# Background copies, marks and one set of sums handed to the POOL queue in a one-core hybrid attention layer

## The chip, the core and the metric

The kernel runs on one core of a Trainium2 chip. The metric is device time in microseconds (us) for one execution of the whole layer. TensorE (PE) does the matmuls and the transposes, VectorE (DVE) and ScalarE (ACT) do elementwise work, GpSimd (POOL) does little but issue transfers, and SyncE (SP) does nothing but issue transfers. Every engine takes its own instructions strictly in its own order. Sixteen DMA engines move the bytes; the profile lists them under two main queues: what SP issues is `q1 hardware_dynamic`, what POOL issues is `q0 software_dynamic`.

## What is computed

One decoder layer on 512 tokens and a model width of 2048, all in float32:

```python
h = _rms_norm(x, g_pre)
proj = h @ w_in                                  # 2048 x 6472
(q_lat, kv_lat, k_rope_raw, gate_mla,
 fq, fk, fv, f_logit, gate_fox) = jnp.split(proj, split_points, axis=-1)
o_mla = _mla_branch(q_lat, kv_lat, k_rope_raw, g_q, w_uq, g_kv, w_ukv, cos, sin) * jax.nn.silu(gate_mla)
o_fox = _fox_branch(fq, fk, fv, f_logit, b_forget) * jax.nn.silu(gate_fox)
o = jnp.concatenate([o_mla, o_fox], axis=-1) @ w_out    # 2048 x 2048
return x + _rms_norm(o, g_post)
```

`_fox_branch` is causal attention with eight heads of 128 and a forget bias. `_mla_branch` is the latent attention: eight heads whose queries come from a normed latent of width 768 through `w_uq` and whose keys and values come from a normed latent of width 512 through `w_ukv`. The projections are the bulk of the work.

## The kernel before

**Exact products from three passes.** A float32 operand is split in two parts, `hi` and `lo` (`split_into`, L134 to L145; for weights `divide`, L272 to L283: ACT casts the high part at L279, DVE subtracts it at L282). A product is three matmuls, `hi*hi`, `hi*lo` and `lo*hi` (`mm3`, L148 to L152). Weights come in chunks of 128x1024 float32 (512 KB); chunk number i is loaded by `load`, split by `divide` and used by PE. `chunk(i)` is called by a product for each chunk in turn: it loads up to four chunks ahead (six in the latent heads) and divides up to two ahead. Raw chunks lie in three buffers in the latent heads and in six in the last products; `whi` and `wlo` have three buffers each.

**Seven products instead of eight.** The large projections (values, latents, gates, the value part of `w_ukv`, and `w_out`) are cut in blocks of 2x2, and sums and differences of weight blocks let seven block products do the work of eight. The sums of weights are called t7, t5, t6 and t4. They are made by transfers, not by an engine: a copy of one block from DRAM to a scratch tensor in DRAM, and then a transfer that adds the second block to it. A few sums are not made ahead. For these ("late"), `load` fetches the two blocks into two tiles, `raw` and `second` (L250), and `join` (L265 to L270) adds them on DVE just ahead of the split. For `w_out` the late one is t5, used by the products `g5`, 0 and `g5`, 1 in four chunks each.

**The background list.** `bg` holds the sums to be made, in order: eight narrow ones (512 KB) for the values, eight for the latents, eight for the gates, four for the value part of `w_ukv`, and twelve wide ones (1 MB, t7, t6 and t4 for four blocks) for `w_out`. `paced` (called by a product at each 128-row step of a chunk, "tile" in this text) counts tiles; each time the count reaches the pace (twice the pace for a wide sum) it calls `add_step(n)`, which does three things: it adds the second block to sum n-1 (POOL, L320), copies the first block of sum n (SP, L324), and writes a mark, 16 numbers out of the weight tile that PE is about to use, into the place of sum n+1 (SP, L326). The mark orders the copy of n+1 behind it, and so keeps the background work in step with the matmuls. In this kernel SP's queue holds the loads of `raw` (L242 and L259), the copies, the marks and the fetches of operands (L985), in one order.

**The latent heads** (L1590 on, `for p in range(4)`). For each p: `mla_q(p)` (six tiles, three PSUM banks of tag `pj`, of which there are four), then at p 0 the first of the products for the values, `up_product("p1", ...)`, into two banks `A`, then `mla_k(p)` (four tiles, two banks of `pj`), then scores and values of two heads. Steps of attention are queued in `todo` and are interleaved with the matmuls by `pump`. At p 2 operand blocks a11 and a12 of the output projection are fetched, at p 3 they are divided (`divisions`, at the head of `todo`). After the loop the a11 blocks of the last four heads' part are split (`head_steps(j, ("a11",), ...)`, j 2 and 3), and the output projection begins with the product `p1`, 0. Its products run in the order p1, p1, p2, p4, p4, q6, g5, g7, q6, g5, g7, g3, g3, p2 (block column 0 or 1); the order of the instructions on each engine is settled by a scheduler when the kernel is built.

**Scratch slots.** `slot` takes one of 28 general buffers of 4 KB per partition; operands, gates, and in the output projection also the `second` tiles are kept there.

Of the kernel before, what the change touches and what calls it, by code (L numbers as in the profile page):

```python
# [16 lines left out]
ALU = mybir.AluOpType  # L17
# [49 lines left out]
def tile_hybrid_layer(  # L67
# [16 lines left out]
    nc = tc.nc  # L84
    pe, act, dve, pool = nc.tensor, nc.scalar, nc.vector, nc.gpsimd
# [14 lines left out]
    def slot(name, dt=F32, shape=(P, 2, S)):  # L100

        return sp.tile(list(shape), dt, tag="s", name=name)

    def bank(tag, name, bufs):
        return ps.tile([P, 512], F32, tag=tag, name=name, bufs=bufs)

    def proj_bank(name):
        return bank("pj", name, 4)
# [23 lines left out]
    def in_order(*instructions):  # L132

        for i in instructions:  # L134
            tc.keep_in_program_order(i)
# [88 lines left out]
    def raw_tile(i):  # L224
        if deep and deep[1] <= i < deep[2] and (i - deep[1]) % (DEEP + 3) < DEEP:
            return deep[0].tile([P, 1024], F32, tag="raw", name=f"raw{i}", bufs=DEEP)
        if i in up_chunks:
            return slot(f"raw{i}", shape=(P, 1024))
        if i <= prods["g7", "v"][-1] and i % 5 < 2:
            return vr.tile([P, 1024], F32, tag="raw", name=f"raw{i}", bufs=2)  # L230
        pool = more[0] if more and (i - more[1]) % 6 < 3 else wp
        return pool.tile([P, 1024], F32, tag="raw", name=f"raw{i}", bufs=3)

    def load(i, small=None):

        w, cols, k, n, width = chunks[i]
        assert state["step"] >= needs.get(i, -3) + 2
        if cols is None:

            raw = raw_tile(i)  # L240
            for a, b in alike(raw, w):
                nc.sync.dma_start(a, b)  # L242
            raws[i] = raw
            if k is not None:
                if seconds:
                    pool, bufs = seconds
                    second = pool.tile([P, 2, 512], F32, tag="second", name=f"second{i}", bufs=bufs)
                else:
                    second = slot(f"second{i}")
                nc.sync.dma_start(second, k)  # L250
                raws[i] = raw, second.rearrange("p k c -> p (k c)")
            return
        if i < 2:
            raw = slot(f"raw{i}", shape=(P, 1024))
        else:
            raw = raw_tile(i)
        v = raw[:, : n * width].rearrange("p (k c) -> p k c", k=n)
        for at, off, cnt in cols:
            (nc.sync if cnt >= P or small is None else small).dma_start(  # L259
                v[:, :, at : at + cnt],  # L260
                w[0, k * P : (k + n) * P, off : off + cnt].rearrange("(k p) c -> p k c", p=P),
            )
        raws[i] = raw
# [41 lines left out]
    bg = []  # L305

    def alike(to, w):

        if len(w.shape) == 4:
            to = to.rearrange("p (k h x) -> p k h x", k=2, h=4)  # L310
            return [(to[:, k], w[:, k]) for k in range(2)]
        return [(to if len(w.shape) == 2 else to.rearrange("p (k c) -> p k c", k=2), w)]

    def add_step(n, mark):


        if n > 0:
            to, _, second = bg[n - 1]
            for a, b in alike(to, second):
                pool.dma_start(a, b, accum_op=ALU.add)  # L320
        if 0 <= n < len(bg):
            to, first, _ = bg[n]
            for a, b in alike(to, first):
                nc.sync.dma_start(a, b)  # L324
        if n + 1 < len(bg):
            nc.sync.dma_start(bg[n + 1][0][0:1, 0:16], mark)  # L326

    def sum_blocks(g, block, late, width=512, nj=4):

# [14 lines left out]
    prods = {}  # L344
# [62 lines left out]
    for n in ("q0", "p1", "k0", "p2", "q6", "p4", "g7", "q1", "g5", "k1", "g3", "q2", "k2", "q3", "k3"):  # L407
# [5 lines left out]
        p = int(n[1])  # L413
# [128 lines left out]
    todo = deque()  # L542
# [9 lines left out]
    def drain():  # L552
        while todo:
            todo.popleft()()

    def set_pace(n):
        state.update(pace=n, tiles=0)
# [378 lines left out]
    def head_steps(j, names, raw_of, place):  # L936

        return operand_steps("o", j, (o_of[K1[j]], o_of[K2[j]]), names, raw_of, place)
# [49 lines left out]
    def part_fetched(n, of, j):  # L988
        both = oper[n, of][j]
        split_into(both[:, 0], both[:, 1], both[:, 1].bitcast(F32), pin=True)  # L990

    def divisions(n, of):
        return [lambda j=j: part_fetched(n, of, j) for j in range(2 if of == "o" else 4)]
# [144 lines left out]
    def x_block(half, tokens):  # L1138
        def parts(kk, t):
            ts = slice((tokens + t) * P, (tokens + t + 1) * P)  # L1140
            return hh[8 * half + kk][:, ts], hl[8 * half + kk][:, ts]

        return parts
# [10 lines left out]
    def scaled_copy(to, o, t0, col=hcol):  # L1154
        for t in range(2):
            act.mul(to[:, t, :], o[t], col[:, t0 + t : t0 + t + 1])
# [28 lines left out]
    def v_block(name):  # L1185
        return vr.tile([P, 2, S], F32, tag="c", name=name)

    def v_out(c, tokens, half):

        for i in range(2):  # L1190
            to = v_away[2 * half + i].rearrange("p (t c) -> p t c", t=NT)[:, 2 * tokens : 2 * tokens + 2, :]
            pool.dma_start(to, c[:, :, 256 * i : 256 * (i + 1)])

    def two_of(make, name):
        return [make(f"{name}{i}") for i in range(2)]
# [24 lines left out]
    todo.extend([*fs[13:], *rot[:3]])  # L1220
    A = two_of(proj_bank, "va")
    product("p1", "v", x_block(0, 0), A, True, True)
    drain()
    pa, pb = v_block("vpa"), v_block("vpb")
    scaled_copy(pa, A, 0, rcol)
    scaled_copy(pb, A, 2, rcol)
    todo.extend([*x_steps(0), *x_steps(1)])
    fox_g(1, two_of(proj_bank, "fg1"))
    drain()
    todo.extend(rot[3:10])  # L1230
    product("p2", "v", x_block(1, 0), A, False, True)
    drain()
    c11 = v_block("vc11")
    scaled_copy(c11, A, 0, rcol)
    v_out(c11, 0, 0)
# [17 lines left out]
    k = fox_k(0, wholes)  # L1253
# [27 lines left out]
    for p in range(4):  # L1281
        if p:
# [6 lines left out]
            k = fox_k(p, wholes)  # L1289
# [138 lines left out]
    A, A2 = ([proj_bank(f"g{n}{t}") for t in range(2)] for n in "lm")  # L1428
# [102 lines left out]
    def halves(a):  # L1531
        return [a[:, t, :] for t in range(2)]
# [55 lines left out]
    for p in range(4):  # L1588
        q, qw, wholes = mla_q(p)
        if p == 0:  # L1590
            set_pace(3)
            A = two_of(proj_bank, "uA")
            up_product("p1", latent_x(0, 0), A, True)
            p1 = slot("up1")
            for t in range(2):
                act.copy(p1[:, t, :], A[t])
            p1 = halves(p1)
        elif p == 1:
            G = two_of(proj_bank, "uG")
            up_product("g5", operand("g5", "u"), G, True)  # L1600
            sub(up[1, 1], G, halves(up[1, 1]), ALU.add)
        elif p == 2:
            for f in (*fetches("a11", "o"), *fetches("a12", "o")):
                f()
        else:
            todo.extendleft([*divisions("a11", "o"), *divisions("a12", "o")])
        k, kw = mla_k(p, wholes)
        drain()
        heads = [
            Head(  # L1610
                f"m{2 * p + i}", q[i], k[i], None,
                lambda h=2 * p + i: gm[h],
                list(zip(qw[i], kw[i])),
            )
            for i in range(2)
        ]
        enqueue_scores(heads)
        if p == 0:
            up_product("p2", latent_x(1, 0), A, False)
            up[0, 0] = slot("u11")  # L1620
            for t in range(2):
                act.copy(up[0, 0][:, t, :], A[t])
            C = two_of(proj_bank, "uC")
            up_product("q6", operand("q6", "u"), C, True)
            up[0, 1] = slot("u12")
            sub(up[0, 1], C, p1)
            B = two_of(proj_bank, "uB")
            up_product("p4", latent_x(1, 2), B, True)
            up[1, 0] = slot("u21")
            sub(up[1, 0], B, p1, ALU.add)  # L1630
            up_product("g7", operand("g7", "u"), C, False)
            sub(up[1, 0], halves(up[1, 0]), C)
            up[1, 1] = slot("u22")
            sub(up[1, 1], C, p1)
            drain()
        elif p == 1:
            up_product("g3", operand("g3", "u"), G, False)
            sub(up[0, 1], G, halves(up[0, 1]), ALU.add)
        mla_values(p)
# [103 lines left out]
        nc.sync.dma_start(gp[c], g_post[:, out_cols(c)].to_broadcast([P, 512]))  # L1743


    for j in (2, 3):
        for s in head_steps(j, ("a11",), tmp, part_slot):
            s()
    todo.extendleft(head_steps(2, ("a12",), tmp, part_slot))
    A, A2 = ([proj_bank(f"oa{g}{t}") for t in range(2)] for g in range(2))  # L1750
    p1 = [slot(f"p1{g}") for g in range(2)]
# [106 lines left out]
```

## Time and profile before

| what | value |
|---|---|
| median of 3 runs | 903.24 us (901.15 to 906.73) |
| the profiled execution's own time | 902.74 us |
| its span, first to last instruction | 900.7 us |
| PE busy | 883.2 us, 98% of the span, 4486 matmuls |
| DVE busy | 659.6 us, 73% |
| ACT busy | 462.4 us, 51% |
| POOL busy | 72.8 us, 8%, 92 instructions |
| mean granted TensorE clock | 0.994 |
| q1 (SP's transfers) | 184.19 MB, 63.0% of 16 engines' span |
| q0 (POOL's transfers) | 39.85 MB, 21.6% of 16 engines' span |

A busy line gives the time of an engine, its share of the span and its instructions. In a table of stretches each row gives a stretch in us from the span's start, its length, the busy time of each engine with its number of instructions, the granted TensorE clock, the DMA engines' busy share, and GB/s. A row of waits names who waited for whom, with the total, the number of times and the longest, in us. A row of the chain of waits gives start, length and what the end of the kernel hung on at that time.

### The profile page before, as it was taken

The numbers are of one execution on the slowest core, as the hardware profiler recorded it, in microseconds if no ns is written. First come the engines' busy times: TensorE is split into PE (matmuls) and PEld (weight loads), VectorE is DVE, ScalarE is ACT, GpSimd is POOL, SyncE is SP. The second block draws the span as 40 slices with busy tenths as digits, with TensorE's granted clock in tenths as the row PEclk, the third lists the DMA queues.
The fourth block names the chain that finished last, engine by engine and source line by source line (L and its number), as shares of the span: only waits on it lengthen the run. The fifth ranks groups of instructions, "written<-read, shape, count | busy, mean of one in ns | idle before, by whom it ended". The sixth has DMA issues, their size and how long they took to land.

```text
span 900.7 us, 12696 instructions
## 1 busy us (share of the span) xinstructions
PE 883.2 (98%) x4486; PEld 749.3 (83%) x4486; DVE 659.6 (73%) x1106; ACT 462.4 (51%) x841; POOL 72.8 (8%) x92
## 2 busy tenths in 40 slices
PE   9999999999999999999999999999989999999996
PEld 9988888888888888889998998778868888877885
DVE  4679995458556545586588898979757895988786
ACT  6944443334343433435545565558454776636383
POOL 0110110001212111000000000000000000000021
PEclk9999999999999999999999999999989999999999
DMA  9998799889999998896899884799995137789879
GB/s 315 283 268 241 201 357 290 249 215 307 286 264 254 261 218 228 240 255 156 312 411 354 315 314 128 173 279 245 227 204 153 61 107 224 239 310 315 263 216 254
DMA packets 139235, 225.07 MB, mean 250 GB/s; under 512 B 16898, under 2 KB 68892, under 8 KB 138148
## 3 DMA queue, kind: packets, MB, share of 16 engines
q1 hardware_dynamic: 124660, 184.19, 63.0%
q0 software_dynamic: 13776, 39.85, 21.6%
q8 instruction: 35, 0.57, 0.2%
q10 hardware_dynamic: 736, 0.22, 0.1%
q14 instruction: 28, 0.23, 0.1%
HBM read 209.53 MB, written 69.22 MB: 309 GB/s over the span
## 4 chain that ended last, share of the span: by engine, by line
PE 85%; DVE 6%; DMA 5%; ACT 2%; issue 1%; SPq 0%; DVEq 0%; ACTq 0%
PE fq L150 3%; PE fk L150 3%; PE fk L152 3%; PE fk L151 3%; PE fq L152 3%; PE fq L151 3%; PE in L612 3%; PE fg L150 3%; PE fg L152 3%; PE fg L151 3%; PE sm L655 2%; PE oa L152 2%; PE sf L655 2%; PE oa L150 2%; PE oa L151 2%; DVE wlo L282 2%
## 5 line engine op out<-in xcount | busy, mean ns | idle before, releaser
L282 DVE TENSOR_TENSOR wlo<-raw,whi 128x1024 fp32r<-128x1024 f32 (+3 forms) x220 | 260.8, 1188 | 142.5 <-ACT whi L279 135.5
L279 ACT CAST whi<-raw 128x1024 fp32r<-128x1024 f32 (+3 forms) x220 | 224.4, 1023 | 242.5 <-PE fk L151 35.3
L150 PE MATMUL fk<-h,whi 128*128 128x512 f32 x128 | 52.5, 410 | 0.0
L150 PE MATMUL fq<-h,whi 128*128 128x512 f32 x128 | 50.8, 397 | 0.0
L150 PE MATMUL fg<-h,whi 128*128 128x512 f32 x128 | 50.3, 393 | 0.0
L152 PE MATMUL fk<-h,wlo 128*128 128x512 f32 x128 | 50.2, 392 | 0.0
L151 PE MATMUL fk<-h,whi 128*128 128x512 f32 x128 | 50.1, 392 | 0.0
L152 PE MATMUL fq<-h,wlo 128*128 128x512 f32 x128 | 50.0, 390 | 0.0
L151 PE MATMUL fq<-h,whi 128*128 128x512 f32 x128 | 49.9, 390 | 0.0
L152 PE MATMUL fg<-h,wlo 128*128 128x512 f32 x128 | 49.9, 390 | 0.0
L151 PE MATMUL fg<-h,whi 128*128 128x512 f32 x128 | 49.8, 389 | 0.0
L673 ACT ACTIVATE pf<-pf,stf 128x128 f32<-128x128 f32 (+3 forms) x32 | 18.0, 563 | 61.5 <-DVE stf L664 61.5
L269 DVE TENSOR_TENSOR raw<-raw,second 128x1024 f32<-128x1024 f32 x32 | 39.0, 1218 | 1.8 <-DMA second<-in_w_out_dram 1.8
L612 PE MATMUL in<-whi,h 128*128 128x328 f32 x128 | 30.0, 321 | 0.0
L150 PE MATMUL mq<-ln,whi 128*128 128x512 f32 x72 | 29.8, 417 | 0.0
L151 PE MATMUL mq<-ln,whi 128*128 128x512 f32 x72 | 28.9, 402 | 0.0
L152 PE MATMUL mq<-ln,wlo 128*128 128x512 f32 x72 | 28.9, 401 | 0.0
L152 PEld LDWEIGHTS fk<-h,wlo 128*128 128x128 f32 x128 | 24.0, 188 | 5.5
L152 PEld LDWEIGHTS fq<-h,wlo 128*128 128x128 f32 x128 | 24.0, 188 | 5.3
L152 PEld LDWEIGHTS fg<-h,wlo 128*128 128x128 f32 x128 | 24.0, 188 | 5.1
L151 PEld LDWEIGHTS fg<-h,whi 128*128 128x128 f32 x128 | 24.1, 188 | 4.8
L150 PEld LDWEIGHTS fg<-h,whi 128*128 128x128 f32 x128 | 24.0, 188 | 4.7
(610 smaller groups left out, 2416.5 us busy)
## 6 DMA issues: line engine op xcount, KB each, us to landing
raw<-in_w_in_dram SPq DMA_DIRECT2D x96, 512.0 KB
raw<-in_w_out_dram SPq DMA_DIRECT2D x32, 512.0 KB
second<-in_w_in_dram SPq DMA_DIRECT2D x24, 512.0 KB
bmg<-awaymg SPq DMA_DIRECT2D x20, 256.0 KB
awaymg<-rmg POOLq DMA_DIRECT2D x8, 512.0 KB, 7.5
raw<-t6v SPq DMA_DIRECT2D x8, 512.0 KB
t7o<-in_w_out_dram SPq DMA_DIRECT2D x4, 1024.0 KB
t7o<-in_w_out_dram POOLq DMA_DIRECT2D x4, 1024.0 KB, 10.8
```

Of the source, the lines that this page charges most:

```text
L150: pe.matmul(o, ah, bh, start=first, stop=False, **kw)
L151: pe.matmul(o, ah, bl, start=False, stop=False, **kw)
L152: pe.matmul(o, al, bh, start=False, stop=last, **kw)
L269: tc.keep_in_program_order(dve.tensor_tensor(out=raw, in0=raw, in1=second, op=ALU.add))
L279: cast = act.copy(hi[:, :m], raw[:, :m])
L282: dve.tensor_tensor(out=lo[:, :m], in0=raw[:, :m], in1=hi[:, :m].bitcast(F32), op=ALU.subtract)
L612: pe.matmul(banks[t][:, :n], a[k][:, tss[t]], b[:, j, :], start=k == 0 and m == 0, stop=k == NK - 1 and m == 2,)
L655: pe.matmul(s[:, :nn], a[:, qs], c[:, :nn], start=(i == 0), stop=(i == len(pairs) - 1))
L673: act.activation(p, p, AF.Exp, bias=st[:, 0:1], scale=unit, accum_out=st[:, 1:2])
```

## The change

Five edits:

1. The copies of the background list (L324) and the marks (L326) are issued by POOL, where the adds (L320) are already; SP keeps the loads and the fetches.
2. For the eight chunks of `g5`, 0 and `g5`, 1 of `w_out` the second block is no longer loaded into a tile of its own and joined on DVE. A transfer issued by POOL adds it to `raw` in SBUF.
3. In the latent heads the pace goes from 3 to 4.5 tiles, which for the wide sums is a step every nine tiles in place of six.
4. At p 0 the second bank of `A` is the `pv` bank in place of a second `pj` bank.
5. The splits of a11, j 2 and 3, move from behind the loop over p to the head of `todo` at p 3, ahead of the divisions.

```diff
@@ load
-            if k is not None:
+            if k is not None and i >= prods["g5", 0][0]:
+                in_order(nc.gpsimd.dma_start(raw.rearrange("p (k c) -> p k c", k=2), k, accum_op=ALU.add))
+            elif k is not None:
                 if seconds:
                     pool, bufs = seconds
@@ add_step
             for a, b in alike(to, first):
-                nc.sync.dma_start(a, b)
+                pool.dma_start(a, b)
         if n + 1 < len(bg):
-            nc.sync.dma_start(bg[n + 1][0][0:1, 0:16], mark)
+            pool.dma_start(bg[n + 1][0][0:1, 0:16], mark)
@@ for p in range(4)
         if p == 0:
-            set_pace(3)
-            A = two_of(proj_bank, "uA")
+            set_pace(4.5)
+            A = [proj_bank("uA0"), bank("pv", "uA1", 1)]
             up_product("p1", latent_x(0, 0), A, True)
@@ the same loop, p 3
-            todo.extendleft([*divisions("a11", "o"), *divisions("a12", "o")])
+            todo.extendleft(
+                [
+                    *divisions("a11", "o"), *divisions("a12", "o"),
+                    *(s for j in (2, 3) for s in head_steps(j, ("a11",), tmp, part_slot)),
+                ]
+            )
@@ behind the loop
-    for j in (2, 3):
-        for s in head_steps(j, ("a11",), tmp, part_slot):
-            s()
     todo.extendleft(head_steps(2, ("a12",), tmp, part_slot))
```

## The prediction, made before the change was run

> **What bounds the kernel now.** First the page: who is busy, and what the end hung on.
>
> ```profile
> PE 883.2 (98%) x4486; PEld 749.3 (83%) x4486; DVE 659.6 (73%) x1106; ACT 462.4 (51%) x841; POOL 72.8 (8%) x92
> ...
> PE 85%; DVE 6%; DMA 5%; ACT 2%; issue 1%; SPq 0%; DVEq 0%; ACTq 0%
> ```
>
> PE is idle for 900.7 - 883.2 = 17.5 us. No matmul is removed, so the change can win only what PE loses to waits, and whatever a lower clock costs after a wait. The second view is who PE waits for.
>
> ```profile
> PE ptm L682 <- DVE stm L664: 4.2, 1, 4.2
> ...
> PE uA L150 <- ACT mw L127: 1.0, 1, 1.0
> PE oa L152 <- DVE boa L140: 0.9, 1, 0.9
> ```
>
> One wait of 4.2 us stands out. It lies in the latent heads. Short stretches around it show that it costs more than its length:
>
> ```profile
> 668.70:673.20 4.50, 0.29 (x4) 0.06 (x2) 1.79 (x4) 1.09 (x2) 0.81 (x1) 0.75 1.11 217
> 673.20:677.70 4.50, 4.50 (x12) 3.65 (x13) 2.83 (x8) 3.16 (x9) 0.00 (x0) 0.50 0.96 197
> ```
>
> PE does nothing for 4.5 - 0.29 = 4.2 us, and for the next 4.5 us it is busy at a granted clock of 0.50, which loses another 2.25 us. Together **6.5 us**. The chain of waits tells why:
>
> ```profile
> 647.94 8.02 DMA t4o<-whi
> 655.98 0.56 SPq L324
> 656.59 0.61 SPq L259
> 657.25 12.99 DMA raw<-in_w_ukv_dram
> 670.34 1.05 ACT whi L279
> 671.41 1.23 DVE wlo L282
> 672.64 0.47 DVE pm L664
> ```
>
> Read it upward. PE waits for the softmax step pm on DVE. DVE stands in its own queue behind a weight split (wlo), that behind a cast, that behind the load of a `w_ukv` chunk. The load was issued at 656.6 and 657.2, behind the background copy (L324) in SP's queue, which stood until a mark (t4o<-whi) had landed, 8.02 us after its issue. And the load then took 12.99 us, with the 1 MB copy ahead of it in the same queue. The third view is SP's own waits:
>
> ```profile
> SPq L259 <- DVE wlo L282: 218.2, 77, 10.2
> ...
> SPq L326 <- ACT whi L279: 62.9, 23, 8.7
> ```
>
> SP mostly waits for raw buffers (218.2 us, harmless while loads are early enough), but 62.9 us go to marks whose weight tile is not yet cast, and every load stands behind them.
>
> **The change part by part.** The sum is made against the profiled execution's own 902.74 us; it stands 0.5 us under the median of 903.24.
>
> *Copies and marks to POOL, a step every nine tiles.* The list has 40 sums, so 40 marks and, as four of the copies take two transfers, 44 copies go from SP to POOL. The nearest price is that of the adds that POOL issues now:
>
> ```profile
> L320 POOL DMA_DIRECT2D t7o<-in_w_out_dram x4 | 4.7, 1163 | 52.2 <-DMA raw<-in_w_uq_dram 28.7 <-DMA t7o<-in_w_out_dram 23.5
> ```
>
> 84 x 1.16 = 97 us on an engine that is busy for 72.8 of 900; all of it lies beside PE. What counts is the load at 656.6. Was its buffer free earlier?
>
> ```profile
> 652.24 0.95 DVE L282 TENSOR_TENSOR wlo<-raw,whi 128x768 fp32r<-128x768 f32 x1
> ```
>
> With three raw buffers the load waits for the split of the chunk three before it, which by its shape (768 wide, a query chunk) is this one; it ends at 653.2. So the load can go at 653.3 and 653.9, 3.3 us earlier. It landed at 657.25 + 12.99 = 670.2, and PE resumed 2.9 us later, at 672.64 + 0.47 = 673.1, after its wait of 4.2; so a landing by 666 costs nothing, and 12 us are left. Even at the old 12.99 it would be 0.9 late, and no copy stands ahead of it any more. I take the whole 6.5 as won; the bounds are 3.3 and 6.5. What is late next is the same load, should it land after 666.
>
> The pace: after the first product of p 0 sets it, the loop has 48 tiles left (14 at p 0, 14 at p 1, 10, 10) and five steps to do. They took 30 tiles, to the second tile of p 2; they will take 45, to the last key tiles of p 3, past 700.
>
> ```profile
> 700.00:720.00 20.00, 20.00 (x102) 16.97 (x101) 17.10 (x42) 14.34 (x36) 0.00 (x0) 1.00 0.17 57
> ...
> 756.88 12.68 SPq L242 DMA_DIRECT2D raw<-t4o  x8
> ```
>
> There the DMA engines have room (0.17), and t4, the last sum and the first one read, is loaded from 756.9 on. So the slower pace costs nothing by itself, and it takes copies out of the full stretch; cover gone would mean an add later than 756, some 40 us off.
>
> *The pv bank at p 0.* A[1] no longer waits for a query bank to be emptied: 1.0 us (the uA row). The first mk product then takes query banks that are free sooner than the third, whose rotation it awaited too:
>
> ```profile
> PEld mk L150 <- DVE rbq L886: 0.5, 1, 0.5
> ```
>
> The pv bank is idle until the first values, after the products are over. **1.4 us** won of 1.5; bounds 0 and 1.5.
>
> *The sum of t5 by transfers into SBUF.* It takes eight loads of `second` off SP and eight joins off DVE. What it loses now is seen in matmuls per 20 us, and what the DMA engines have left in the last column but one:
>
> ```profile
> 780.00:800.00 20.00, 20.00 (x90) 16.57 (x89) 18.05 (x23) 10.27 (x14) 0.00 (x0) 1.00 0.76 248
> 800.00:820.00 20.00, 18.56 (x80) 14.36 (x79) 16.77 (x18) 9.78 (x12) 0.00 (x0) 1.00 0.87 288
> 820.00:840.00 20.00, 20.00 (x90) 16.57 (x89) 17.48 (x21) 9.12 (x14) 0.00 (x0) 1.00 0.95 349
> 840.00:860.00 20.00, 19.94 (x89) 16.02 (x88) 13.17 (x15) 8.94 (x9) 0.00 (x0) 1.00 0.87 281
> ```
>
> Ten matmuls of 90 are missing at 800 to 820: 10 x 20/90 = 2.2 us; one at 840 to 860, 0.2. The reason in the chain: the first `second` lands late, and then join, cast and the next join follow each other at 3.6 us a chunk, where PE takes 12 x 20/90 = 2.7.
>
> ```profile
> 785.10 5.68 SPq L242 DMA_DIRECT2D raw<-in_w_out_dram  x3
> ...
> 791.21 6.80 DMA second<-in_w_out_dram
> 798.11 1.24 DVE raw L269
> ...
> 799.50 1.06 ACT whi L279
> ...
> 801.72 1.23 DVE raw L269
> ...
> DMA to landing us min/median/max: 5.3/8.9/15.4
> ...
> DMA to landing us min/median/max: 7.6/9.4/11.1
> ```
>
> The new wait: POOL's add waits for `raw` to land, behind it in POOL's queue stand only the next adds, since the background is done by then, and the cast waits for the add. From the load at 785.1 to the cast at 799.5 are 14.4 us. The load is bounded by the 6.80 of its neighbour; an add takes 8.9 us in the middle by the background's row (L320, the first of the two) and 9.4 by the only adds into SBUF here, those of x at the end (L1675, 256 KB, the second). 6.8 + 8.9 = 15.7, that is 1.3 us late; with SP's queue rid of four 512 KB loads I expect the load to land in less, and put down 1.0 us for both stages together. Bounds: 0, and 6.8 + 15.4 - 14.4 = 7.8 in each stage. Net **-1.4 us**; DVE's eight joins (1.22 us each) lie beside PE once the chain is gone.
>
> The adds are dearer for the DMA engines than loads:
>
> ```profile
> q1 hardware_dynamic: 124660, 184.19, 63.0%
> q0 software_dynamic: 13776, 39.85, 21.6%
> ```
>
> 0.342% of 16 engines' span for a MB against 0.542%; eight adds of 0.524 MB cost 8 x 0.524 x 0.2% x 900.7 = 7.6 us of all engines more than the loads they replace. From 780 to 860 the shares above leave (0.24 + 0.13 + 0.05 + 0.13) x 20 = 11 us, so they fit. The Trainium skill ("Collectives: The Full Stack", section "The bandwidth ceiling: the fold count and why AG ≠ RS ≠ AR") says that an adding transfer has two reads to make and halves the rate; by that rule an add would cost a second load, an estimate of 8 x 1.6 = 12.9 us in place of 7.6, 1.9 more than is free, and the sum would be 1.9 us higher. The trace's ratio is 1.6, not 2; its q0 holds plain copies too.
>
> *The a11 splits.* DVE in that place:
>
> ```profile
> 721.75 1.29 DVE L140 TENSOR_TENSOR boa<-boa 128x512 fp32r<-128x512 f32 x2
> ...
> 726.27 1.28 DVE L140 TENSOR_TENSOR soa<-gm,soa 128x512 fp32r<-128x512 f32 x2
> ```
>
> PE's first output product waits 0.9 us for the divisions (boa). `extendleft` turns the list round, so the two splits (soa) now come ahead of them: 1.28 us of DVE moves from 726 to a place before 721. At worst the wait grows by 1.3; at best PE order shifts and the 0.9 goes. I take **+0.7**.
>
> Sum: -6.5 - 1.4 - 1.4 + 0.7 = -8.6; 902.74 - 8.6 = **894 us**.
>
> **The rivals.**
>
> *Half of the stall stays* (897.5). The add and the copy of the same step now lie on q0 at once and share the 16 engines with the load; at 668.7 to 673.2 these are full (1.11). Then only SP's 3.3 us are won: 894 + 3.2. For it: the load's 12.99 us also ran beside an add of 1 MB. Against: one copy less is ahead, and 12 us suffice.
>
> *The adds are late* (899). They come 3 us too late in each g5 stage, and the gain there is gone: 894 - 1.0 + 6. For it: 15.7 against 14.4. Against: the adds of x, eight in ten us, landed in 11.1 at most.
>
> *The change does nothing where it counts* (901). SP's loads wait for buffers, not for marks; then 218.2 us of SP's waits speak for loads as late as before, and only the bank helps: 902.74 - 1.4. Against: SP stood at L324, not at L259, before the late load.
>
> *POOL's one queue becomes the bound; slower than before* (915). Add, copy and mark of a step now stand in one queue, and each copy awaits its mark. The narrowest place is the last t6 of the values:
>
> ```profile
> 148.50 1.22 POOL L320 DMA_DIRECT2D t7v<-in_w_in_dram  x1 [24.62 <-DMA t7v<-in_w_in_dram]
> 156.98 0.88 POOL L320 DMA_DIRECT2D t6v<-t7v  x1 [7.26 <-DMA t6v<-in_w_in_dram]
> ...
> 176.08 0.32 SPq L242 DMA_DIRECT2D raw<-t6v  x1
> ```
>
> Two steps are 8.5 us apart, and the load comes 19.1 us after the add's issue. If all three land one behind another, a step takes 8.9 + 10.15 (the longest copy on the chain, below) + 8.02 = 27 us, so the add is issued 18.6 later and lands 8.9 after that: 8.4 us too late, plus 2.25 for the clock; the same queueing makes the adds of g5 5 us late a stage, of the possible 7.8. 894 + 10.6 + 10 = 915. It decides from 8.6 us of new waits on. For it: the mark above took 8.02 us for 64 bytes. Against: 19.1 us at this place hold two thirds of the worst step, and 5.3 us is the shortest landing of an add.
>
> ```profile
> 590.00 10.15 DMA t7o<-in_w_out_dram
> ```
> The Trainium skill ("DMA: Bandwidth & Descriptors", section "SWDGE vs HWDGE vs iDMA") names only one queue for transfers issued by POOL, and the engines take turns between it and the others; by that rule this case is the one that follows if the turns are in order. The page of the profile lists one such queue, q0, too.
>
> **How the numbers follow.** Chances: forecast 0.60 (889 to 898), half of the stall 0.13, late adds 0.11, nothing 0.07, POOL's queue 0.09. The range of 8 in 10 reaches to the other cases on the high side: 887.5 to 902. Its low end is all terms at their best (6.5 + 1.5 + 2.4 + 0.9 = 11.3, 891) and 3.5 us for small waits of 0.2 to 0.5 us a stretch that fewer transfers in SP's queue may also end. About 1% is what a measurement of this kernel can tell from no change, so faster begins at 894.2: some seven tenths of the forecast case, since the gains that the sum leaves out lie on that side, 0.42. Slower begins at 912.3: most of the last rival, 0.07. The rest, 0.51, is within 1%.
>
> **What would show it.** Right: no PE wait on stm near 668, the granted clock at 1.00 in 660 to 680, no uA wait, DVE joins only 24, 90 matmuls per 20 us from 780 to 860. SP's waits on marks gone. Wrong: casts (L279) that wait for a raw that POOL added to, PE waits on od or oa, or loads of t6v behind POOL.

## The result, and the profile after

The changed kernel takes **975.8 us** (median; 974.0 to 980.1) against 902.6 for the kernel before beside it: a ratio of 1.081, with a 95% interval of 1.076 to 1.086. The forecast was 894, in a range of 887.5 to 902. The profiled execution took 976.09 us with a span of 974.0. One execution among all that follow, of the kernel with marks first, took 2275.63 us and is left out of that kernel's ratio. Lines of the changed kernel stand two higher than before: the weight cast is L281, its second part L284, the add L322, the copy L326, the mark L328; L245 is the new add into SBUF.

The page of the changed kernel, engines and the slices of PE:

```profile
PE 902.3 (93%) x4486; PEld 758.2 (78%) x4486; DVE 651.8 (67%) x1098; ACT 462.3 (47%) x841; POOL 135.0 (14%) x184
...
PE   8999999999996787969799999999999989998996
```

PE was idle for 17.5 us and is idle for 974.0 - 902.3 = 71.7 now. Most of it lies in one stretch, the slices of 7s, 6s and 8s: 290 to 490 us, the forget heads. The windows of before (first row) and after (second row) over an equal number of matmuls show what that stretch costs; the columns are length, busy time of each engine with its instructions, granted clock, DMA share, GB/s.

```profile
240.00:480.00 240.00, 239.88 (x1276) 205.61 (x1275) 151.42 (x297) 105.03 (x203) 26.03 (x29) 1.00 0.93 268
```
```profile
240.00:540.00 300.00, 255.13 (x1282) 214.04 (x1282) 147.13 (x304) 100.85 (x200) 53.45 (x71) 0.92 0.78 211
```

The same work takes 60 us more. 45 of them are idle PE; the other 15 are longer matmuls, at a clock of 0.92 in place of 1.00. The DMA engines are less busy than before, not more. This is a stretch of which the prediction said nothing.

Whom PE waits for, and whom ACT waits for, in the changed kernel (total, times, longest):

```profile
PE pvf L150 <- ACT phf L139: 20.5, 5, 9.3
PE sf L657 <- ACT fw L127: 12.9, 2, 7.8
...
PE oa L150 <- ACT boa L139: 3.5, 1, 3.5
```
```profile
ACT whi L281 <- issue: 59.5, 17, 10.3
...
ACT whi L281 <- DMA t7m<-whi: 18.6, 2, 9.6
```

PE waits mostly for small copies on ACT, and ACT stands before a weight cast. In five places the profile names the cause itself, 29.6 us in all: the cast into a `whi` buffer waits until a *mark* that reads this buffer has landed (t7m<-whi is two of them). For the waits put down to "issue" it names nothing; the place below fits a mark, and with marks that read another tile most of the 59.5 us go (13.1 are left, shown below; the kernel before has 17.3). The place in the timelines of POOL, ACT and PE:

```profile
326.97 1.15 POOL L322 DMA_DIRECT2D t7m<-in_w_in_dram  x1 [6.46 <-DMA t7m<-in_w_in_dram]
327.69 1.89 POOL L953 DMA_DIRECT2D awayoa<-gf  x2
328.90 1.19 POOL L328 DMA_DIRECT2D t6m<-whi  x1
340.71 0.72 POOL L326 DMA_DIRECT2D t6m<-in_w_in_dram  x1 [10.61 <-DMA t6m<-whi]
344.99 0.90 POOL L322 DMA_DIRECT2D t6m<-t7m  x1 [3.56 <-DMA t6m<-in_w_in_dram]
```
```profile
340.49 1.04 ACT L281 CAST whi<-raw 128x1024 fp32r<-128x1024 f32 x1 [9.85 <-issue]
...
342.06 0.96 ACT L139 CAST phf<-ptf 128x512 fp32r<-128x512 f32 x2
```
```profile
342.69 0.79 PE L150 MATMUL pvf<-phf,fv2h 128*128 128x512 f32 x1 [8.02 <-ACT phf L139]
```

Read them together. POOL's add at 326.97 has waited 6.46 us for its copy to land, and the mark behind it could not be issued before 328.90. It then lands behind the add and two away transfers of the same queue: POOL's copy, which waits for it, goes at 340.71. ACT's cast starts at 340.49, in the same moment, after standing 9.85 us. Behind the cast in ACT's queue stands the split of the probabilities (phf), and PE stands 8.02 us for it. A mark moves 64 bytes. The view of line L328 gives the casts that waited for marks, and the time from a mark's issue to its landing:

```profile
ACT whi L281: 29.6, 5
...
DMA to landing us min/median/max: 1.6/6.0/11.7
```

The order on POOL, add, mark, copy, is not that of the code (add, copy, mark): in most steps the program's scheduler put the mark behind the next step's add. Such a step costs two landings one behind the other, the copy's and then the mark's: some 18 us in the stretch above (326.97 to 344.99).

The Trainium skill ("DMA: Bandwidth & Descriptors", section "SWDGE vs HWDGE vs iDMA") recommends plain transfers from SP or ACT and leaves to GpSimd those that add or cast. The runs below agree: the copies and marks are plain transfers, 84 in all, and moving the marks alone from SP to POOL cost 56 us, the copies alone 4.

The 668 us stall itself is gone, as forecast: no wait for stm is left in PE's list, and the work that had it, now between 730 and 750 us, runs without a gap and at full clock.

```profile
730.00:750.00 20.00, 20.00 (x104) 16.81 (x103) 13.52 (x27) 10.08 (x24) 2.09 (x3) 1.00 0.87 185
```

### The profile page after: what moved, and what is told of

The parts are those of the page before. It is cut to its first block, busy times and chain, and to the rows that moved or that the text cites. A ratio compares the mean times of both kernels' runs of the same rounds, so it can differ in the third digit from the quotient of the medians.

```text
span 974.0 us, 12647 instructions
## 1 busy us (share of the span) xinstructions
PE 902.3 (93%) x4486; PEld 758.2 (78%) x4486; DVE 651.8 (67%) x1098; ACT 462.3 (47%) x841; POOL 135.0 (14%) x184
## 4 chain that ended last, share of the span: by engine, by line
PE 47%; DMA 4%; DVE 2%; ACT 2%; issue 1%; DVEq 0%; ACTq 0%; POOLq 0%
DMA raw<-in_w_out_dram 4%; PE sm L657 3%; PE mq L150 2%; PE mq L152 2%; PE mq L151 2%; PE oa L150 2%; PE oa L151 2%; PE oa L152 2%; PE od L151 1%; PE od L152 1%; PE od L150 1%; PE gl L150 1%; DVE wlo L284 1%; PE gl L151 1%; PE gl L152 1%; PE gcl L152 1%
## 5 line engine op out<-in xcount | busy, mean ns | idle before, releaser
L284 DVE TENSOR_TENSOR wlo<-raw,whi 128x1024 fp32r<-128x1024 f32 (+3 forms) x220 | 260.8, 1189 | 224.6 <-ACT whi L281 218.1
L281 ACT CAST whi<-raw 128x1024 fp32r<-128x1024 f32 (+3 forms) x220 | 224.2, 1022 | 333.6 <-issue 59.5
L150 PE MATMUL fk<-h,whi 128*128 128x512 f32 x128 | 54.0, 422 | 0.0
L150 PE MATMUL fq<-h,whi 128*128 128x512 f32 x128 | 52.4, 409 | 0.0
L151 PE MATMUL fk<-h,whi 128*128 128x512 f32 x128 | 51.3, 401 | 0.0
L151 PE MATMUL fq<-h,whi 128*128 128x512 f32 x128 | 51.3, 401 | 0.0
L271 DVE TENSOR_TENSOR raw<-raw,second 128x1024 f32<-128x1024 f32 x24 | 29.2, 1218 | 3.3 <-DMA second<-in_w_in_dram 3.3
L150 PEld LDWEIGHTS fq<-h,whi 128*128 128x128 f32 x128 | 25.1, 196 | 4.7
L150 PEld LDWEIGHTS fk<-h,whi 128*128 128x128 f32 x128 | 25.1, 196 | 4.6
L151 PEld LDWEIGHTS fq<-h,whi 128*128 128x128 f32 x128 | 24.9, 195 | 4.6
L151 PEld LDWEIGHTS fk<-h,whi 128*128 128x128 f32 x128 | 25.1, 196 | 4.1
```

Source lines behind the costliest of these rows:

```text
L150: pe.matmul(o, ah, bh, start=first, stop=False, **kw)
L151: pe.matmul(o, ah, bl, start=False, stop=False, **kw)
L271: tc.keep_in_program_order(dve.tensor_tensor(out=raw, in0=raw, in1=second, op=ALU.add))
L281: cast = act.copy(hi[:, :m], raw[:, :m])
L284: dve.tensor_tensor(out=lo[:, :m], in0=raw[:, :m], in1=hi[:, :m].bitcast(F32), op=ALU.subtract)
```

## The experiments

Each ratio is against the kernel before, run beside the changed one; its median was 900.4 to 901.7 us.

My theory (M in the expectations): a mark reads `whi`, so it holds one of the three `whi` buffers until it lands, and on POOL it lands late. The rivals: Q, the copies on POOL's queue, or their load on the DMA engines; R, a changed order of work.

**Marks back on SP**, all else as after:

```diff
-            pool.dma_start(bg[n + 1][0][0:1, 0:16], mark)
+            nc.sync.dma_start(bg[n + 1][0][0:1, 0:16], mark)
```


> The kernel after with the marks alone given back to SP; the copies stay on POOL, and so do all other edits. Theory M (a mark reads 64 bytes of whi and so holds one of the three whi buffers until it lands; on POOL it is issued behind the add and the copy of its step and lands 5 to 12 us late; the next cast into that buffer stands, ACT's queue behind it, and then PE): PE's loss of some 60 us between 260 and 480 us falls to the 3 us of before, so 912 to 922, and the casts' waits for marks (t6m<-whi, t7m<-whi) go. Theory Q (it is the copies on POOL's one queue, or their load on the DMA engines, that make it late): hardly anything comes back, 960 or more. Theory R (the edits shift the order of work, not the queue): 960 or more as well.

Measured: 915.9 us, 1.016 (1.014 to 1.019). 60 of the 73 us come back, as M said, and the heads are as they were:

```profile
240.00:480.00 240.00, 239.28 (x1272) 204.61 (x1271) 149.59 (x301) 101.77 (x199) 39.10 (x47) 1.00 0.92 263
```

**Only the marks to POOL**, all else as before:

> The kernel before with the marks alone issued by POOL; copies stay on SP, nothing else is changed. Theory M: the mark stands in POOL's queue behind an add that waits for its copy, so it holds its whi buffer as it does in the kernel after; 930 to 960. Theory Q (copies on POOL are the cause): 900 to 906, since no copy moves.

Measured: 957.8 us, 1.063 (1.058 to 1.068): +56 us, with no copy moved. Q and R fall as causes of the large loss. The timelines of POOL and ACT in this kernel show a wait of M with its name:

```profile
343.90 0.89 POOL L320 DMA_DIRECT2D t6m<-t7m  x1 [12.89 <-issue]
344.45 0.87 POOL L326 DMA_DIRECT2D t7u<-whi  x1
```
```profile
350.12 1.04 ACT L279 CAST whi<-raw 128x1024 fp32r<-128x1024 f32 x1 [9.67 <-DMA t7u<-whi]
```

The add stands 12.89 us, the mark goes behind it, and the cast waits 9.67 us, until 350.12, for that mark.

But M is not all of these 56 us. Here the copies are still on SP, where they wait for the late marks, and the loads stand behind the copies. The first row is one of twelve such rows of SP; together they are 291 us, against 63 in the kernel before. The second is casts that wait for a late load. The third is the stall of the prediction, which was 4.2 us long:

```profile
SPq L324 <- DMA t4o<-whi: 43.0, 3, 16.3
...
ACT whi L279 <- DMA raw<-in_w_in_dram: 40.3, 14, 6.1
...
PE ptm L682 <- DVE stm L664: 13.2, 1, 13.2
```

Of PE's idle time some 20 us lie in the forget heads (200 to 500 us) and some 27 in the latent heads (600 to 800, against 7 before). So late marks cost about the same in both kernels, but in part by different ways; the changed kernel, whose SP queue has no copies, can't lose by this one.

**The mark reads another tile.** As after, but ACT puts the 16 numbers into a small tile of eight buffers and the mark reads that:

```diff
+            seal = cst.tile([1, 16], F32, tag="seal", name=f"seal{n}", bufs=8)
+            act.copy(seal, mark)
-            pool.dma_start(bg[n + 1][0][0:1, 0:16], mark)
+            pool.dma_start(bg[n + 1][0][0:1, 0:16], seal)
```


> The kernel after, marks and copies still on POOL, but ACT copies the 16 numbers of whi into a small tile of eight buffers, and the mark reads that tile. It adds 40 tiny copies on ACT and leaves POOL's queue as late as it was; what it takes away is that a late mark holds a whi buffer. Theory M: PE's 60 us in the fox heads go, 915 to 922. If it is instead the lateness of POOL's queue itself (late sums, late loads) or the load on the DMA engines: 960 or more.

Measured: 958.5 us, 1.063 (1.061 to 1.065). By its number M missed, and the rival of a queue that is late by itself (960 or more) was nearly right. By its windows and by PE's list of waits M was half right: between 240 and 460 us PE hardly stands, and then it stands once, for 41.6 us. The casts' waits put down to "issue" are back to less than before the change.

```profile
240.00:460.00 220.00, 219.88 (x1135) 186.70 (x1134) 130.92 (x286) 94.60 (x206) 44.99 (x60) 1.00 0.83 216
460.00:520.00 60.00, 17.12 (x120) 16.42 (x119) 11.46 (x13) 5.87 (x7) 7.65 (x11) 0.63 0.84 264
```
```profile
PE gbl L150 <- ACT whi L281: 41.6, 1, 41.6
...
ACT whi L281 <- issue: 13.1, 10, 1.7
```

ACT's and POOL's timelines around it (the mark is L330 here), and the row of DVE's sums in the view of the tile rog:

```profile
509.94 0.59 ACT L1463 COPY lat<-gl 128x512 f32<-128x512 f32 x1 [47.36 <-DMA awayog<-rog]
```
```profile
454.12 0.87 POOL L322 DMA_DIRECT2D t6o<-t7o  x1 [9.05 <-DMA t6o<-in_w_out_dram]
...
465.90 0.71 POOL L326 DMA_DIRECT2D t4o<-in_w_out_dram  x1 [10.40 <-DMA t4o<-seal]
472.93 0.85 POOL L322 DMA_DIRECT2D t4o<-t6o  x1 [6.31 <-issue]
...
493.10 1.05 POOL L955 DMA_DIRECT2D awayog<-rog  x1
```
```profile
L965 DVE TENSOR_TENSOR rog<-gf,rog x4: 681/684/693, 438.9 to 506.6; 128x512 f32<-128x512 f32 x4
```

No mark holds a `whi` buffer, yet POOL still works off its steps at some 19 us each (454.12 to 472.93), waiting for a mark and then for a copy. The transfer that takes finished rows (rog) out of their slot stands behind these steps and goes at 493.10; the first such rows were summed at 438.9. ACT needs the slot for `lat`. So the theory was too narrow: holding `whi` is the way by which the late queue reaches PE first, and the late queue is the cause. Take the one way, and it reaches PE by the next.

**Marks first.** As after, with each step's mark ahead of its add and copy, and the order pinned:

```diff
+        if n + 1 < len(bg):
+            in_order(pool.dma_start(bg[n + 1][0][0:1, 0:16], mark))
         if n > 0:
 ...
-                pool.dma_start(a, b, accum_op=ALU.add)
+                in_order(pool.dma_start(a, b, accum_op=ALU.add))
 ...
-                pool.dma_start(a, b)
+                in_order(pool.dma_start(a, b))
-        if n + 1 < len(bg):
-            pool.dma_start(bg[n + 1][0][0:1, 0:16], mark)
```


> The kernel after, all transfers still on POOL, but each step's mark is issued first and the order mark, add, copy is pinned; in the kernel after the order that came out is add, mark, copy, so that a mark stands behind an add that waits for a copy to land, and the next copy waits for that mark (about 20 us a step). If the place in the queue is the cause, marks land in 2 to 4 us, a step needs some 10 us, casts and away transfers are in time, and 55 to 60 us come back: 912 to 922. If marks on POOL's queue are dear wherever they stand: 950 or more.

Measured: 938.2 us (936.7 without the long execution), 1.040 (1.037 to 1.044), between both expectations. POOL's timeline (L320 the mark, L324 the add, L328 the copy):

```profile
290.25 1.19 POOL L324 DMA_DIRECT2D t7m<-in_w_in_dram  x1 [5.38 <-DMA t7m<-in_w_in_dram]
290.98 1.16 POOL L328 DMA_DIRECT2D t6m<-in_w_in_dram  x1
291.68 0.97 POOL L320 DMA_DIRECT2D t6m<-whi  x1
300.25 0.86 POOL L324 DMA_DIRECT2D t6m<-t7m  x1 [7.60 <-DMA t6m<-in_w_in_dram]
```

A step costs 10 us as expected, one landing in place of two. The other half of the expectation failed: marks were to land in 2 to 4 us, but the median is 6.4 (longest 12.9), since each still follows the copy of the step before by 0.7 us in the one queue. So `whi` is still held. The pinned order also keeps the first four copies from running ahead at the start (below, "the copies alone"): PE is busy for 18.94 of the first 20 us, as in the kernel before, against 16.37 in the changed kernel. Some 3 of the 38 us won are that.

**Both remedies.** Marks first, and from the small tile:

> The kernel after with both remedies: each step's mark first and the order pinned (steps of 10 us), and the mark reads ACT's copy of the 16 numbers (no whi held). With the first alone 938 was measured, with the second alone 958. If whi held and POOL's backlog are the two halves of the loss, PE loses some 3 us between 200 and 480 (23 with the first alone), no wait for an away transfer appears, and what is left is the g5 sums, the a11 splits and the copies: 914 to 920. If something else on POOL's queue is dear, about 938 stays.

Measured: 923.9 us, 1.026 (1.021 to 1.031), 4 us above the expected range. PE's list of waits has neither `fw` nor `phf` any more. Of the forget heads one wait is left that counts, the second row; the first, in the latent heads, resembles one that the copies make by themselves (below, "the copies alone").

```profile
PE mk L150 <- ACT mw L127: 4.2, 1, 4.2
PE pvf L150 <- ACT fv3h L139: 2.3, 1, 2.3
```

So 52 of the 60 us are found: 38 by taking away POOL's backlog (976 to 938, with the 3 at the start), and 14 more by freeing `whi` (938 to 924). The two are not separate: a shorter backlog also means that a mark which holds `whi` is issued sooner. The difference of 8 us to marks on SP wasn't taken apart.

**The pace alone**, as before with `set_pace(4.5)` in the latent heads:

> The kernel before with only the pace in the latent heads slower (a step every nine tiles of 2 x 4.5 where it was every six of 2 x 3); marks and copies stay on SP. The prediction's reading (the stall at 668 comes from the load of w_ukv behind a mark and a copy in SP's queue, and a slower pace costs nothing): with fewer steps in the stretch some or all of the 6.5 us go, 895 to 899. Rival (the loads wait for their raw buffers and not for marks): 901 to 903, no change.

Measured: 896.9 us, 0.9947 (0.9931 to 0.9962). The stall goes, by the window in which it lay:

```profile
660.00:680.00 20.00, 20.00 (x101) 17.02 (x100) 13.49 (x40) 12.81 (x35) 0.55 (x1) 1.00 0.83 189
```

**The copies alone** to POOL:

> The kernel before with only the background copies issued by POOL; marks stay on SP. Theory M (only what holds whi costs): the copies are free in the heads; the first ones, now issued at 2.6 to 5 us beside the loads of x, cost the 3.2 us by which the first 20 us are longer in the kernel after; the stall near 668 shrinks or goes, since the load no longer stands behind the copy: 898 to 905. Theory Q (the copies on POOL's one queue are dear by themselves): 915 or more.

Measured: 905.7 us, 1.0041 (1.0026 to 1.0056). They cost 4 us net. The first 20 us, before and here:

```profile
0.00:20.00 20.00, 18.94 (x124) 18.34 (x125) 8.85 (x15) 13.54 (x38) 2.10 (x12) 1.00 0.94 305
```
```profile
0.00:20.00 20.00, 16.11 (x94) 15.47 (x95) 6.43 (x11) 9.64 (x25) 7.82 (x18) 0.91 0.97 268
```

Four copies that have no mark to wait for come at the front of POOL's queue, are issued at 2.6 to 5.1 us and share the DMA engines with the loads of x; PE waits 2.8 us for x, which it does not before. And at 591 us a load of `w_ukv` runs beside an add and a copy of POOL (issued at 591.25 and 595.40) and takes 15.31 us. The row of the chain of waits, whose next steps are its cast, its split and mw, and PE's wait at their end:

```profile
591.02 15.31 DMA raw<-in_w_ukv_dram
```
```profile
PE uA L150 <- ACT mw L127: 4.3, 1, 4.3
```

The stall at 668 is all but gone here too (0.3 us), which pays for part of it. That POOL's two transfers made the load at 591 us long is read from their times; no run takes them away.

**The pv bank alone:**

> The kernel before with only the pv bank for the second half of uA. The prediction's term was -1.4 us (900). The trace of the kernel with marks given back to SP speaks against it: ACT's next weight cast stands 7.33 us for the uA product that now runs ahead of the emptying of the query banks, the emptying stands behind that cast, and mk waits 3.1 us for it: +4 to +6, 905 to 908.

Measured: 901.2 us, 1.0008 (0.9991 to 1.0025): no difference that can be told. My expectation of +4 to +6 was wrong: the late `mw` that I put on the bank shows with the copies alone (the last row above) and not with the bank alone.

**The sums of t5 alone:**

> The kernel before with only w_out's last sum (t5) made by adding transfers into the raw tiles. The prediction's term was -1.4 us (901), with a bound of +7.8 in each stage. From the trace of after, where PE loses 11.4 us between 860 and 920 against 2.7 in the same work before: +8 to +9, 911. Rival: that those adds were late only because background work of the latent heads had been pushed behind them; then 900 to 903.

Measured: 908.9 us, 1.0087 (1.0056 to 1.0118), +7.5 us. The adds on POOL and the casts on ACT in the first stage:

```profile
786.91 1.24 POOL L245 DMA_DIRECT2D raw<-in_w_out_dram  x1 [117.83 <-DMA raw<-in_w_out_dram]
...
803.35 1.21 POOL L245 DMA_DIRECT2D raw<-in_w_out_dram  x1 [8.42 <-DVE wlo L284]
```
```profile
796.92 1.05 ACT L281 CAST whi<-raw 128x1024 fp32r<-128x1024 f32 x1 [4.57 <-DMA raw<-in_w_out_dram]
800.86 1.05 ACT L281 CAST whi<-raw 128x1024 fp32r<-128x1024 f32 x1 [2.89 <-DMA raw<-in_w_out_dram]
804.92 1.05 ACT L281 CAST whi<-raw 128x1024 fp32r<-128x1024 f32 x1 [3.01 <-DMA raw<-in_w_out_dram]
...
812.38 1.04 ACT L281 CAST whi<-raw 128x1024 fp32r<-128x1024 f32 x1 [5.89 <-DMA raw<-in_w_out_dram]
```

The first cast follows its add by 10.0 us and comes early enough (799.5 before). But the casts follow each other by 4 us, where PE needs one each 2.7, and the fourth chunk's add, issued at 803.35, lets its cast go only at 812.38. The issue of the adds is not what spaces the first three: the second and third were issued at 789.36 and 793.73, and landed one behind another. The fourth was held back, by a wait that the profile ends with DVE's split of the second chunk. The landings of these adds, in the view of the tile raw:

```profile
DMA to landing us min/median/max: 8.9/10.9/13.6
```

**The a11 splits alone:**

> The kernel before with only the two a11 splits moved into the list of the last latent pair. The prediction's term was +0.7 us (903.3). From the trace of after, where PE stands 3.5 us for boa from ACT at a clock that then falls to 0.91: +3 to +4, 906.

Measured: 906.4 us, 1.0055 (1.0033 to 1.0078), +4.9 us. ACT's timeline, before (the first fence) and with the edit:

```profile
714.03 2.20 ACT L139 CAST boa<-boa 128x512 fp32r<-128x512 f32 x4
```
```profile
719.65 1.05 ACT L279 CAST whi<-raw 128x1024 fp32r<-128x1024 f32 x1 [4.72 <-PE mk L151]
...
721.88 1.14 ACT L139 CAST soa<-gm 128x512 fp32r<-128x512 f32 x2
722.93 2.17 ACT L139 CAST boa<-boa 128x512 fp32r<-128x512 f32 x4
```

The four casts boa had a gap on ACT to themselves. Behind the a11 splits (soa) they miss it, stand behind a weight cast that waits for PE, and come 9 us later.

**The a11 splits behind the divisions** in the same list:

> The kernel before with the a11 splits in the same list, but behind the divisions of a11 and a12 and not ahead of them. My reading of the early version (+5.0): ACT's four casts boa lose their idle place at 714 to 718, stand behind a weight cast that waits for PE till 719.7, and end at 725.1, so PE waits 3.5 us for them. With the divisions first they get it back: 900 to 903.5. If splitting a11 in this stretch is dear whatever the order: 905 to 907.

Measured: 901.7 us, 1.0003 (0.9985 to 1.0020). Within the interval, the order in the list was all of the cost.

**The pace and the bank**, on the kernel before:

```diff
-            set_pace(3)
-            A = two_of(proj_bank, "uA")
+            set_pace(4.5)
+            A = [proj_bank("uA0"), bank("pv", "uA1", 1)]
```


> The kernel before with the slower pace and the pv bank, the two edits that by themselves did not cost. By the single runs (-4.8 and about 0): 895 to 898. If the bank's 1.4 us of the prediction appears once the stall is gone: 894 to 896.

Measured: **896.3 us**, 0.9944 (0.9923 to 0.9964). It beats both kernels; from the pace alone (896.9) it can't be told apart. No wait of PE for stm or uA is left, and PE is idle for 893.5 - 881.0 = 12.5 us.

## Why the prediction was wrong

The single edits measured: marks +56.3, copies +4.1, pace -4.8, bank -0.4, t5 sums +7.5, a11 splits +4.9; in sum +67.6 of the 73.3 measured together. That the sum comes so near is in part luck, since the marks alone lose their time partly on SP's loads; taken out of the changed kernel, the marks are worth 60. Against the prediction's steps:

- **Marks to POOL at nothing: the step that failed.** "84 x 1.16 = 97 us ... all of it lies beside PE" priced the issue on POOL. It asked who waits for the moved mark on SP, the queue that it left, and not what the mark itself holds nor what it stands behind on the queue that it joined. The mark reads a tile of three buffers; on POOL it waits behind an add that waits for a copy, and lands behind both. Both were to be had from the trace of before: in the very row that priced them, four of POOL's adds stood 23.5 us for the landing of their copies, and SP's row for L326 says that a mark waits for the cast of `whi`, so it reads that tile. In place of nothing the marks cost 56 us alone, and 60 of the 73 in the changed kernel.
- **The stall at 668, -6.5.** Reading and direction right: it goes with the slower pace alone (-4.8), and with the copies moved. The size stood 1.7 us too high. The pace alone was enough; the move to POOL was not needed for it.
- **Copies at nothing.** Measured +4.1 net, though they also win the stall, so some 9 us were missed, an estimate from 4.1 and the 4.8 of the pace. The prediction saw that they would share the DMA engines with loads ("half of the stall stays"), but put that at 668 only. It came at the start, where copies without a mark ran ahead, and, it seems, at 591.
- **pv bank, -1.4.** Measured -0.4, within 0.9991 to 1.0025. Too small to tell.
- **t5 sums, -1.4.** The sign failed; the price, +7.5, is about one of the two bounds of 7.8. The term was sized for the first chunk alone (14.4 against 15.7 us), and the first chunk was in time. The pitch of the next three, 4 us and then 7.5, decided: the adds landed one behind another, in 10.9 us in the middle where 8.9 was taken, and the fourth was issued late. What spaces the landings, and why the fourth add had to wait, stays open.
- **a11 splits, +0.7.** Measured +4.9. The step counted DVE's 1.28 us; the cost was ACT's order, four casts that lost their gap. It named the swap in the list, and looked at one engine of two.

The rival "POOL's one queue becomes the bound; slower than before" named the cause and the sign, at 915 and a chance of 0.09. Its place was wrong (the last t6 of the values; the losses lie mostly in the forget heads), and so its price: it counted sums that come late for their loads, where the marks hold back the casts. Of what was to be seen, the stall's end, the full clock and the 24 joins came; 90 matmuls per 20 us in the g5 stages did not, and of the uA wait 0.8 us stayed. Of its signs of being wrong, casts that wait for a raw that POOL added to (26.0 us, 8 times) and PE's waits on od and oa came, but they belong to the small terms; no sign named the marks.

## What to carry to other kernels

In these traces a transfer that reads a tile was a user of its buffer until it landed, even one of 64 bytes (the cast that waits 9.67 us): ask what it stands behind on the queue that it joins, and which engine waits for that buffer. On an in-order queue, put what others wait for ahead of what waits for landings, and pin that order if the schedule is made by a program. When a split or cast is moved, read the gaps of every engine that it touches, not only of the one whose time it takes.

## What the runs showed of the hardware

A transfer of 64 bytes issued by POOL took 1.6 us at best, 6.0 in the middle and 11.7 at most, with transfers of 512 KB and 1 MB in the same queue; marks issued first but 0.7 us behind such a copy did no better (6.4 in the middle). By a rule of the Trainium skill ("DMA: Bandwidth & Descriptors", section "Anatomy of one DMA — SWDGE (gpsimd) path") such a transfer would take about 2.0 us, an estimate; the shortest is near it and the median is three times as long. Eight adds of 512 KB into SBUF landed in 8.9 to 13.6 us. And waits of up to 9 us that come again and again cost more than their length: between 240 and 540 us of the changed kernel the granted clock was 0.92, where it was 1.00 over the same work before, and the longer matmuls are about a quarter of that stretch's loss.
